# Self-attention of one decoder layer: both chunks of a query block handled together, products with the values and the query norms each in one run of column groups

## The chip, the cores and the metric

The kernel runs on one core of one Trainium2 chip. The metric is the device time of one execution in microseconds, from the runtime's own clock; the profile's span is the time from the first to the last instruction of the program within such an execution. PE is the matmul engine, PEld its weight load, DVE the vector engine, ACT the scalar engine, POOL the GpSimd engine, SP the engine that issues most DMAs.

## The reference

One inference step of one decoder layer for 256 prompt positions (two chunks of 128) and 8 sample requests of one position each, all in fp32. What is computed in sequence:

```
proj = rms_norm(x, g_mix) @ w_in                  # q | k | v | z | x,B,C | dt
q, k = rms_norm per head (16 and 4 heads of 64)
attn = sliding-window attention (window 128, a learned sink per head)
         prompt: each chunk sees itself and the chunk before, masked
         sample: one query per request against 128 cached rows and itself
ssd  = depthwise conv, SiLU, chunked state-space scan, gated norm
x = x + concat(attn, ssd) @ w_out
x = x + cross_attention(x, 256 memory tokens)     # 4 heads of 128
x = x + (silu(conv(gate)) * conv(value)) @ w_down # up-projection 2048 -> 2 x 5632
```

The prompt's attention, which the change concerns, is for each head `p = softmax(q k^T / 8 + mask, with the sink in the denominator)` and `o = p v`.

## The kernel before, in words

Positions lie along the free axis (256 prompt and 8 sample positions, 264 columns) and features along the partitions. All large products are done three times in a one-pass format: weights and inputs are split into a high and a low part, and `mm3` (L97 to L100) multiplies high by high, high by low and low by high into one accumulation. `weights` (L72) loads 128x1024 of a matrix, ACT casts the high part `whi` (L85), DVE subtracts it to get the remainder `wlo` (L86). `proj` (L102) does pairs of 128 output rows: 96 such products ("projection products" in what follows) for a pair of blocks with 2048 inputs.

The input projection comes in 26 pairs (`in_pair`, L350): keys, values, four pairs of queries, then the convolution's blocks (B and C, then x), then z. A pair's accumulators are two PSUM banks of tag "mm" (three banks), and from the sixteenth pair on every other one takes two of tag "t" (two banks, L355). The other tags are "s", "x" and "y" with a bank each.

Small products that are not of this kind are in fp32: the profile shows two records for each such product, one for a transpose. They are written for a few heads at a time and a scheduler that runs when the program is built puts them between the projection products, on each engine in one fixed order. That order, and not the code's, is what the chip runs; an engine that comes to an instruction whose inputs are not there stands still.

The query norm (L561 to L564): for each of 8 query blocks `j` (two heads each) ACT squares the block, and a product with a 128x32 selection matrix `nw` sums the squares of the two heads. Block `j` writes 32 partitions of bank "s" (column group `j % 4`), blocks 0 to 3 and 4 to 7 adding into the same four groups. `qn`, two transposes, a square root and a reciprocal make the factors `rqs` of it (L577 to L586).

The prompt's attention `attn_prompt` (L510) is called for each of 8 query blocks and treats each chunk `c` by itself: scores of both heads against 128 or 256 keys (L516, bank "s"), mask added by DVE (L519), maximum (L522), three small steps with the norm's factors and the sink (L524 to L526), exponentials on ACT (L527, L529), denominator (L531, L532), scaling (L534), transposes on PE (L539, shown as L271) into a "t" bank, a copy by ACT (L541, tile `pt`), the products with the values (L545: head 0 writes partitions 0 to 63, head 1 64 to 127 of another "t" bank) and a copy into `attn` (L547). The scores' tile `pe` has three buffers, shared under the tag "h0" with the sample's attention and the old states `h0` of `ssd_sample`; `pt` has two.

After it `attn_sample` (L591) does the 8 sample requests: scores in one bank "s" (L611), softmax (L615 to L623), a transpose into a "t" bank (L625), DVE's copy of it (L626), products with the cached values (L633), a copy (L635), a transpose and a diagonal product into the other "t" bank (L637, L638), and DVE's sums (L641, L645). `ssd_prompt` (L717) is the scan of the prompt, `ssd_sample` (L786) that of the sample requests: for each of 32 tiles a load of an old state on POOL's queue (L793), a product (L794) and a sum (L795) on DVE.

Of the kernel before, what the change touches and what calls it, by code (L numbers as in the profile page):

```python
# [7 lines left out]
F32 = mybir.dt.float32  # L8
F32R = mybir.dt.float32r
AF = mybir.ActivationFunctionType  # L10
ALU = mybir.AluOpType
AX = mybir.AxisListType
# [4 lines left out]
TP, TS = 256, 8  # L17
# [30 lines left out]
def hybrid_decoder_step_kernel(ctx: ExitStack, tc: tile.TileContext, I, O):  # L48
    nc = tc.nc
    V, S, P, PE = nc.vector, nc.scalar, nc.gpsimd, nc.tensor  # L50
# [9 lines left out]
    def psum(tag):  # L60
        return ps.tile([128, 512], F32, tag=tag, name=tag, bufs=banks[tag])

    def T3(pool, n, dt=F32, tag=None, name=None, bufs=None):
        return pool.tile([128, n, T], dt, tag=tag, name=name or tag, bufs=bufs)
# [191 lines left out]
    def pc(name, i=0, n=1):  # L256
        o = _PC[name][0]
        return par[:, o + i:o + i + n]
# [6 lines left out]
    maskb = cst[:, C_MASK:C_MASK + 256]  # L265
# [3 lines left out]
    def tr(out, in_):  # L269
        k = in_.shape[0]  # L270
        return PE.transpose(out, in_, cst[0:k, C_ID:C_ID + k])  # L271
# [59 lines left out]
    mp = mix.enter_context(tc.tile_pool(name="mp", bufs=1))  # L331
# [9 lines left out]
    def t32(name):  # L341
        return t6[:, next(t6n), :]
# [74 lines left out]
    vn = mp.tile([128, 2, 2, 128], F32, name="vn")  # L417
    p = psum("y")
# [20 lines left out]
    q = t32("q")  # L439
# [16 lines left out]
    p = psum("x")  # L456
# [5 lines left out]
    p = psum("x")  # L462
# [44 lines left out]
    nsink = mp.tile([128, 16], F32, name="nsink")  # L507
    V.tensor_scalar(out=nsink, in0=pc("sink_p", 0, 16), scalar1=-1.0, scalar2=None, op0=ALU.mult)

    def attn_prompt(j, rq, nrq):  # L510
        pp = j // 4
        for c in range(2):
            nk = 128 * (c + 1)
            p = psum("s")
            s3 = p[:, 0:2 * nk].rearrange("p (h k) -> p h k", h=2)
            PE.matmul(s3, qT[:, j, c * 128:c * 128 + 128], kbd[:, pp, :, 0:nk], start=True, stop=True)  # L516
            e = mp.tile([128, 2, 256], F32, tag="h0", name="pe", bufs=3)
            ev = e[:, :, 0:nk]
            V.tensor_tensor(out=ev, in0=s3, in1=maskb[:, 256 - nk:256].unsqueeze(1).broadcast_to([128, 2, nk]), op=ALU.add)  # L519
            st = mp.tile([128, 8], F32, tag="st", name="st", bufs=4)  # L520
            mx, den, es = st[:, 0:2], st[:, 2:4], st[:, 4:6]
            V.tensor_reduce(out=mx, in_=ev, op=ALU.max, axis=AX.X)  # L522

            V.tensor_tensor(out=mx, in0=mx, in1=nrq[:, c, :], op=ALU.mult)  # L524
            V.tensor_tensor(out=mx, in0=mx, in1=nsink[:, 2 * j:2 * j + 2], op=ALU.min)
            V.tensor_tensor(out=es, in0=mx, in1=pc("sink_p", 2 * j, 2), op=ALU.add)  # L526
            S.activation(out=es, in_=es, func=AF.Exp)  # L527
            for h in range(2):
                S.activation(out=e[:, h, 0:nk], in_=e[:, h, 0:nk], func=AF.Exp, scale=rq[:, c, h:h + 1], bias=mx[:, h:h + 1],  # L529
                             accum_out=den[:, h:h + 1])  # L530
            V.tensor_tensor(out=den, in0=den, in1=es, op=ALU.add)  # L531
            V.reciprocal(out=den, in_=den)  # L532
            for h in range(2):
                V.tensor_scalar(out=e[:, h, 0:nk], in0=e[:, h, 0:nk], scalar1=den[:, h:h + 1], scalar2=None, op0=ALU.mult)  # L534
            p = psum("t")
            nb = c + 1
            for h in range(2):
                for kb in range(nb):
                    tr(p[:, (h * nb + kb) * 128:(h * nb + kb) * 128 + 128], e[:, h, kb * 128:kb * 128 + 128])  # L539
            pt = mp.tile([128, 4, 128], F32, tag="bc", name="pt", bufs=2)  # L540
            S.copy(out=pt[:, 0:2 * nb, :], in_=p[:, 0:2 * nk].rearrange("p (a q) -> p a q", q=128))  # L541
            o = psum("t")
            for h in range(2):
                for kb in range(nb):
                    PE.matmul(o[64 * h:64 * h + 64, 0:128], vn[:, kb, pp, 64 * h:64 * h + 64], pt[:, h * nb + kb, :],  # L545
                              start=kb == 0, stop=kb == nb - 1)
            marks["attn"] = S.copy(out=attn[:, j, c * 128:c * 128 + 128], in_=o[:, 0:128])  # L547

    marks = {}

    qsq = [T3(apool, 4, tag="R", name=f"qsq{i}", bufs=4) for i in range(2)]
    nw = zz[:, :, 512:544]
# [6 lines left out]

            S.activation(out=qsq[j // 4][:, j % 4, :TP], in_=qT[:, j, :TP], func=AF.Square)  # L560
    pq = psum("s")  # L561
    for d in range(2):
        for j in range(4):
            PE.matmul(pq[32 * j:32 * j + 32, 0:TP], nw[:, d, :], qsq[d][:, j, :TP], start=d == 0, stop=d == 1)  # L564
    cpc = mp.tile([128, 24, 8], F32, name="cpc")
    ctmp = mp.tile([128, 2, TP], F32, tag="c", name="ctmp", bufs=2).rearrange("p a b -> p (a b)")[:, :192].rearrange("p (a b) -> p a b", b=8)

# [10 lines left out]
    pq = psum("x")  # L578
# [8 lines left out]
    for j in range(8):  # L587
        d = 2 * (j // 4)
        attn_prompt(j, rqs[:, :, j % 4, d:d + 2], nrqs[:, :, j % 4, d:d + 2])
# [109 lines left out]
    for c in range(2):  # L699
        p = psum("x")  # L700
# [4 lines left out]
    for w, XT in enumerate((BT, CT)):  # L705
        p = psum("x")
# [71 lines left out]
    p = psum("x")  # L778
# [196 lines left out]
    pts = [t.rearrange("p (m a q) -> p m a q", m=2, a=2) for t in (vp[:, 1024:2048], pp1[:, 0:1024])]  # L975
# [164 lines left out]
    p = psum("y")  # L1140
# [43 lines left out]
    for pi, (wh, wl) in enumerate(weights(I["w_co"][0])):  # L1184
        wh, wl = (w.rearrange("p (k c) -> p k c", c=512) for w in (wh, wl))
        for k in range(2):
            h = 2 * pi + k
# [7 lines left out]
    for u in range(1, 4):  # L1195
        proj([I["w_co"][u]], [(OH, OL)], lambda m, pm, u=u: x2_ev(4 * u + m, pm), nb=4,
             tag=[cyc[(4 * (u - 1) + m) % 5] for m in range(4)])
# [255 lines left out]
def build(shapes):  # L1453

    import concourse.bacc as bacc

    nc = bacc.Bacc("TRN2", target_bir_lowering=False, num_devices=1)
    ins = {n: nc.dram_tensor(f"in_{n}_dram", s, dt, kind="ExternalInput").ap() for n, (s, dt) in shapes.items()}
    outs = {n: nc.dram_tensor(f"out_{n}_dram", s, F32, kind="ExternalOutput").ap() for n, s in _OUTS}
    with tile.TileContext(nc, schedule_with_timeline_sim=True) as tc:  # L1460
        hybrid_decoder_step_kernel(tc, ins, outs)
    return nc
# [10 lines left out]
```

## Time and profile before

| what | value |
|---|---|
| device time, three runs | 1409.09, 1410.20, 1411.24 us (median 1410.2) |
| device time of the profiled execution | 1409.84 us |
| its span | 1407.8 us |
| L545, products with the values | 96 records, 8.8 us of busy time |
| L564, query norm | 16 records, 2.3 us of busy time |
| granted TensorE clock | 1.00 |

A line of the timeline gives the start, the duration, the engine, the line, what is written and read, the size and the number of records merged; a bracket at its end tells how long the engine had been idle and what ended that. A record of a matmul is longer than what it costs, since matmuls are pipelined and their records overlap: what one costs is read from the start of one to the start of the next.

### The profile page before, as it was taken

How to read it: one execution, taken by the hardware profiler on the slowest of the kernel's cores; microseconds unless marked ns; L12 is line 12 of the kernel's file. 1: busy time of each engine (PE TensorE's matmuls, PEld its weight loads, DVE VectorE, ACT ScalarE, POOL GpSimd, SP SyncE). 2: the span in 40 equal slices, each digit the busy share in tenths (PEclk: the TensorE clock that was granted, in tenths of full speed). 3: DMA queues.
4: the chain of work that ended last, by engine and by line, in shares of the span. 5: the costliest groups of instructions: out<-in, count | busy, mean ns of one | idle time of the engine just before them, and what ended most of it. 6: DMA issues, size and time to landing. Idle time of an engine off the chain costs nothing.

```text
span 1407.8 us, 29049 instructions
## 1 busy us (share of the span) xinstructions
PE 1399.9 (99%) x11525; PEld 1367.7 (97%) x11525; DVE 1047.8 (74%) x1909; ACT 764.1 (54%) x1255; POOL 96.2 (7%) x282
## 2 busy tenths in 40 slices
PE   9999999999999999999999999999999999999999
PEld 8998899999999999899999999999999999999999
DVE  7869879999997784468777775777577757765664
ACT  7557765656545554566565553555355535543432
POOL 0000001221010000020010010001000100000000
PEclk9999999999999999999999999999999999999999
DMA  8864357777776667666576765676567656656554
GB/s 300 290 191 134 118 178 251 223 249 249 243 225 236 188 224 246 247 232 192 178 235 235 238 230 182 212 242 228 181 211 229 206 182 198 199 175 191 183 188 139
DMA packets 90775, 298.33 MB, mean 212 GB/s; under 512 B 12304, under 2 KB 17808, under 8 KB 90128
## 3 DMA queue, kind: packets, MB, share of 16 engines
q1 hardware_dynamic: 84704, 277.34, 60.2%
q0 software_dynamic: 5504, 18.88, 4.2%
q8 instruction: 90, 1.47, 0.4%
q14 instruction: 45, 0.37, 0.1%
q10 hardware_dynamic: 432, 0.27, 0.1%
HBM read 280.77 MB, written 16.23 MB: 211 GB/s over the span
## 4 chain that ended last, share of the span: by engine, by line
PE 97%; DMA 1%; DVE 1%; issue 0%; ACT 0%; ACTq 0%; SPq 0%; DVEq 0%
PE mm L99 21%; PE mm L98 21%; PE mm L100 21%; PE t L99 10%; PE t L98 10%; PE t L100 10%; PE s L516 1%; PE t L271 1%; PE y L750 1%; PE t L545 1%; DMA cpast<-in_cpast_dram 1%; PE y L766 0%; DMA xT<-in_xT_dram 0%; PE t L242 0%; PE x L271 0%; PE x L1045 0%
## 5 line engine op out<-in xcount | busy, mean ns | idle before, releaser
L85 ACT CAST whi<-wraw 128x1024 fp32r<-128x1024 f32 x442 | 462.5, 1048 | 526.1 <-PE mm L99 271.2
L86 DVE TENSOR_TENSOR wlo<-wraw,whi 128x1024 fp32r<-128x1024 f32 x442 | 542.1, 1227 | 232.1 <-ACT whi L85 229.7
L98 PE MATMUL mm<-x2h,whi 128*128 128x264 f32 x704 | 199.8, 284 | 0.0
L98 PE MATMUL t<-x2h,whi 128*128 128x264 f32 x704 | 199.7, 284 | 0.0
L99 PE MATMUL t<-x2l,whi 128*128 128x264 f32 x704 | 199.7, 284 | 0.0
L99 PE MATMUL mm<-x2l,whi 128*128 128x264 f32 x704 | 199.6, 284 | 0.0
L100 PE MATMUL t<-x2h,wlo 128*128 128x264 f32 x704 | 199.5, 283 | 0.0
L100 PE MATMUL mm<-x2h,wlo 128*128 128x264 f32 x704 | 199.3, 283 | 0.0
L99 PE MATMUL mm<-hl,whi 128*128 128x264 f32 x704 | 198.7, 283 | 0.0
L100 PE MATMUL mm<-hh,wlo 128*128 128x264 f32 x704 | 198.2, 283 | 0.0
L98 PE MATMUL mm<-hh,whi 128*128 128x264 f32 x704 | 197.2, 284 | 0.0
L98 PE MATMUL mm<-xh,whi 128*128 128x264 f32 x608 | 176.3, 292 | 0.0
L99 PE MATMUL mm<-xl,whi 128*128 128x264 f32 x608 | 173.8, 287 | 0.0
L100 PE MATMUL mm<-xh,wlo 128*128 128x264 f32 x608 | 172.0, 288 | 0.4 <-DVE wlo L86 0.4
L99 PEld LDWEIGHTS t<-x2l,whi 128*128 128x128 f32 x704 | 132.5, 188 | 0.0
L99 PEld LDWEIGHTS mm<-x2l,whi 128*128 128x128 f32 x704 | 132.5, 188 | 0.0
L99 PEld LDWEIGHTS mm<-hl,whi 128*128 128x128 f32 x704 | 132.5, 188 | 0.0
L98 PEld LDWEIGHTS t<-x2h,whi 128*128 128x128 f32 x704 | 132.5, 188 | 0.0
L98 PEld LDWEIGHTS mm<-x2h,whi 128*128 128x128 f32 x704 | 132.4, 188 | 0.0
L100 PEld LDWEIGHTS t<-x2h,wlo 128*128 128x128 f32 x704 | 132.2, 188 | 0.0
L100 PEld LDWEIGHTS mm<-x2h,wlo 128*128 128x128 f32 x704 | 132.1, 188 | 0.0
L100 PEld LDWEIGHTS mm<-hh,wlo 128*128 128x128 f32 x704 | 131.9, 188 | 0.0
(461 smaller groups left out, 2917.9 us busy)
## 6 DMA issues: line engine op xcount, KB each, us to landing
wraw<-in_w_up_dram SPq DMA_DIRECT2D x176, 512.0 KB, 4.2
wraw<-in_w_in_dram SPq DMA_DIRECT2D x102, 512.0 KB, 4.8
wraw<-in_w_dn_dram SPq DMA_DIRECT2D x88, 512.0 KB, 4.2
wraw<-in_w_out_dram SPq DMA_DIRECT2D x48, 512.0 KB, 4.5
h<-in_h_dram POOLq DMA_DIRECT2D x32, 256.0 KB, 4.6
hn<-in_h_dram SPq DMA_DIRECT2D x16, 512.0 KB, 4.8
out_state_s_dram<-hn POOLq DMA_DIRECT2D x16, 512.0 KB, 3.9
e<-dram_la SPq DMA_DIRECT2D x16, 256.0 KB, 4.6
```

The costliest lines, as they stand in the source:

```text
L85: S.copy(out=hi, in_=x)
L86: V.tensor_tensor(out=lo, in0=x, in1=hi.bitcast(F32), op=ALU.subtract)
L98: PE.matmul(out, wh, xh, start=start, stop=False)
L99: PE.matmul(out, wh, xl, start=False, stop=False)
L100: PE.matmul(out, wl, xh, start=False, stop=stop)
L271: return PE.transpose(out, in_, cst[0:k, C_ID:C_ID + k])
L516: PE.matmul(s3, qT[:, j, c * 128:c * 128 + 128], kbd[:, pp, :, 0:nk], start=True, stop=True)
L545: PE.matmul(o[64 * h:64 * h + 64, 0:128], vn[:, kb, pp, 64 * h:64 * h + 64], pt[:, h * nb + kb, :], start=kb == 0, stop=kb == nb - 1)
L750: PE.matmul(y[o:o + 64, (h // 2) * 128:(h // 2) * 128 + 128], xdt[:, h, :], es[h // 4][:, h % 4, :], start=True, stop=True)
```

## The change

The change touches `attn_prompt` and the query norm. Both chunks of a query block go through together: the two score products write different banks ("s" for the first chunk, "y" for the second by the text `"ys"[c]`: "y" for c = 0, "s" for c = 1), the small steps on maximum, sink and denominator are done once for both chunks (four columns instead of two), the transposed probabilities of both chunks are held in the two `pt` buffers, and the products of both chunks with the values write one "t" bank and are issued in one run, six products without another one between. ACT copies the result once. The query norm's eight products are issued in one run as well, blocks 4 to 7 first. In the changed kernel the lines behind L510 move: scores L520, products with the values L556, query norm L578, and everything from `attn_sample` on by 21 (L615 becomes L636, L794 becomes L815).

```diff
     def attn_prompt(j, rq, nrq):
         pp = j // 4
+        st = mp.tile([128, 3, 2, 2], F32, tag="st", name="st", bufs=4)
+        mx, den, es = st[:, 0], st[:, 1], st[:, 2]
+        ev = []
         for c in range(2):
             nk = 128 * (c + 1)
-            p = psum("s")
+            p = psum("ys"[c])
...
-            V.tensor_tensor(out=mx, in0=mx, in1=nrq[:, c, :], op=ALU.mult)
-            V.tensor_tensor(out=mx, in0=mx, in1=nsink[:, 2 * j:2 * j + 2], op=ALU.min)
-            V.tensor_tensor(out=es, in0=mx, in1=pc("sink_p", 2 * j, 2), op=ALU.add)
-            S.activation(out=es, in_=es, func=AF.Exp)
+            V.tensor_reduce(out=mx[:, c, :], in_=e, op=ALU.max, axis=AX.X)
+            ev.append(e)
...
+        V.tensor_tensor(out=mx, in0=mx, in1=nrq, op=ALU.mult)
+        V.tensor_tensor(out=mx, in0=mx, in1=sink(nsink), op=ALU.min)
+        V.tensor_tensor(out=es, in0=mx, in1=sink(pc("sink_p", 0, 16)), op=ALU.add)
+        S.activation(out=es, in_=es, func=AF.Exp)
...
-            o = psum("t")
-            for h in range(2):
-                for kb in range(nb):
-                    PE.matmul(o[64 * h:64 * h + 64, 0:128], vn[:, kb, pp, 64 * h:64 * h + 64], pt[:, h * nb + kb, :],
-                              start=kb == 0, stop=kb == nb - 1)
-            marks["attn"] = S.copy(out=attn[:, j, c * 128:c * 128 + 128], in_=o[:, 0:128])
+            pts.append(pt)
+        o = psum("t")
+
+        def pv(c):
+            nb = c + 1
+            return [PE.matmul(o[64 * h:64 * h + 64, c * 128:c * 128 + 128], vn[:, kb, pp, 64 * h:64 * h + 64], pts[c][:, h * nb + kb, :],
+                              start=kb == 0, stop=kb == nb - 1) for h in range(2) for kb in range(nb)]
+
+        with tc.issue_after(pv(1)[0].ins):
+            pv(0)
+        marks["attn"] = S.copy(out=attn[:, j, 0:TP], in_=o[:, 0:TP])
...
-    for d in range(2):
+    def norm(d, j):
+        return PE.matmul(pq[32 * j:32 * j + 32, 0:TP], nw[:, d, :], qsq[d][:, j, :TP], start=d == 1, stop=d == 0)
+
+    with tc.issue_after(norm(1, 3).ins):
+        for j in range(3):
+            norm(1, j)
         for j in range(4):
-            PE.matmul(pq[32 * j:32 * j + 32, 0:TP], nw[:, d, :], qsq[d][:, j, :TP], start=d == 0, stop=d == 1)
+            norm(0, j)
```

The built program's order shows it. First PE's order at the products with the values of one query block; `pt` are the transposed probabilities, `vn` the values, numbers tell tiles apart. Before:

```order
L545 MATMUL t_1175<-pt_1173,vn_488 64x128 x2
L271 MATMUL t_1195<-cst_72,pe_1181 128x128 x4
L516 MATMUL s_1262<-kv_339,attn_347 128x256
L100 MATMUL mm_1889<-xh0_78,wlo_1893 128x264
...
L100 MATMUL mm_1889<-xh0_78,wlo_1899 128x264
L545 MATMUL t_1202<-pt_1200,vn_488 64x128 x4
L271 MATMUL t_1224<-cst_72,pe_1210 128x128 x2
L516 MATMUL s_1287<-kv_339,attn_347 128x512
```

Now:

```order
L100 MATMUL mm_1817<-xh0_78,wlo_1827 128x264
L556 MATMUL t_1182<-pt_1180,vn_488 64x128 x4
L556 MATMUL t_1182<-pt_1171,vn_488 64x128 x2
L520 MATMUL s_1241<-kv_339,attn_347 128x512
L520 MATMUL y_1281<-kv_339,attn_347 128x256
L98 MATMUL mm_1817<-xh0_78,whi_1826 128x264
```

The two runs, 25 projection products apart, are one, into one bank. Eight such runs stand in the changed program, the last after projection product 1287 (counting L98 to L100 from the start), where the last of before stood after 1026; the norm's eight products stand in one run too, where before six stood together and two alone.

Second, PE's order at the second half of the sample requests' attention; `es_e` are their probabilities, `vc` the cached values, `oss` the result before its transpose, `dgs` a diagonal. Before, at projection products 1149 to 1194:

```order
L271 MATMUL t_1570<-cst_72,es_e_1565 128x128
L98 MATMUL mm_2494<-xh1_80,whi_2563 128x264
...
L633 MATMUL s_1575<-vc_343,zz_345 32x128 x16
L100 MATMUL mm_2631<-xh0_78,wlo_2635 128x264
...
L271 MATMUL t_1594<-cst_72,oss_1592 128x128
L638 MATMUL t_1594<-dgs_1573,cst_72 128x128
L98 MATMUL mm_2631<-xh0_78,whi_2640 128x264
```

Now, at 1333 to 1344; `s_1471` are the scores:

```order
L632 MATMUL s_1471<-kcT_341,zz_345 32x129 x16
L99 MATMUL mm_2806<-xl1_81,whi_2875 128x264
...
L100 MATMUL mm_2806<-xh1_80,wlo_2876 128x264
L271 MATMUL t_1498<-cst_72,es_e_1493 128x128
L654 MATMUL s_1503<-vc_343,zz_345 32x128 x16
L271 MATMUL t_1522<-cst_72,oss_1520 128x128
L659 MATMUL t_1522<-dgs_1501,cst_72 128x128
L744 MATMUL s_2704<-CT_1535,BT_1534 128x128
L98 MATMUL t_2942<-xh0_78,whi_2946 128x264
```

The four steps of the sample, spread over 120 projection products from its scores on, now stand within 11, and the projection products behind them write the other bank of the same tag "t". 24 products on, PE transposes `xs0` into the bank that `x_2723` held (row `L271 MATMUL x_2767`).

Third, DVE's order behind DVE's copy of that transpose; `h0` are old states, `x_2723` the bank that PE wants next. Before:

```order
L626 COPY zz_345<-t_1570 128x4x4x8
...
L794 TENSOR_TENSOR h0_3165<-h0_3165,cb_3159 128x512
L670 SCALAR_TENSOR_TENSOR c_2617<-u2_545,par_71,c_2617 128x256
L795 TENSOR_REDUCE ych_2205<-h0_3165 128x4
L670 SCALAR_TENSOR_TENSOR c_2617<-u3_547,par_71,c_2617 128x256
L86 TENSOR_TENSOR wlo_2882<-wraw_2879,whi_2881 128x1024
L641 TENSOR_TENSOR tso_1597<-t_1594,kv_339 128x64 x2
```

Now:

```order
L647 COPY zz_345<-t_1498 128x4x4x8
L691 SCALAR_TENSOR_TENSOR c_2929<-u3_547,par_71,c_2929 128x256
L693 SCALAR_TENSOR_TENSOR xs2_2125<-xs2_2125,c_2929 128x2x256
L815 TENSOR_TENSOR h0_3089<-h0_3089,cb_3087 128x512
L815 TENSOR_TENSOR h0_3093<-h0_3093,cb_3087 128x512
L816 TENSOR_REDUCE ych_2133<-h0_3089 128x4
L816 TENSOR_REDUCE ych_2133<-h0_3093 128x4
L662 TENSOR_TENSOR tso_1525<-t_1522,kv_339 128x64 x2
L766 TENSOR_TENSOR xw_2730<-x_2723,de_535 128x512
L746 TENSOR_TENSOR s_2704<-s_2704,cst_72 128x128
L666 TENSOR_TENSOR tso_1525<-tso_1525,t_1522 128x128
```

The first steps of the scan (L766, L746) stand directly behind the sample's sums and the old states' first products, and the load of `h0_3093` waits for PE's transpose of the sample's probabilities (`t_1498`), whose buffer it takes over.

More of the change, by code (lines that the diff above doesn't have):

```diff
@@ L511, in attn_prompt @@
         pp = j // 4
+        st = mp.tile([128, 3, 2, 2], F32, tag="st", name="st", bufs=4)
+        mx, den, es = st[:, 0], st[:, 1], st[:, 2]
+        ev = []
         for c in range(2):
             nk = 128 * (c + 1)
-            p = psum("s")
+            p = psum("ys"[c])
             s3 = p[:, 0:2 * nk].rearrange("p (h k) -> p h k", h=2)
             PE.matmul(s3, qT[:, j, c * 128:c * 128 + 128], kbd[:, pp, :, 0:nk], start=True, stop=True)
-            e = mp.tile([128, 2, 256], F32, tag="h0", name="pe", bufs=3)
@@ L518, in attn_prompt @@
[L518 to L522, printed above, removed]
-            V.tensor_tensor(out=mx, in0=mx, in1=nrq[:, c, :], op=ALU.mult)
-            V.tensor_tensor(out=mx, in0=mx, in1=nsink[:, 2 * j:2 * j + 2], op=ALU.min)
@@ L526, in attn_prompt @@
-            V.tensor_tensor(out=es, in0=mx, in1=pc("sink_p", 2 * j, 2), op=ALU.add)
-            S.activation(out=es, in_=es, func=AF.Exp)
-            for h in range(2):
[L529 to L532, printed above, removed]
-            for h in range(2):
-                V.tensor_scalar(out=e[:, h, 0:nk], in0=e[:, h, 0:nk], scalar1=den[:, h:h + 1], scalar2=None, op0=ALU.mult)
@@ L535, in attn_prompt, with sink @@
-            p = psum("t")
+            e = mp.tile([128, 2, 256], F32, tag="h0", name="pe", bufs=3)[:, :, 0:nk]
+            V.tensor_tensor(out=e, in0=s3, in1=maskb[:, 256 - nk:256].unsqueeze(1).broadcast_to([128, 2, nk]), op=ALU.add)
+            V.tensor_reduce(out=mx[:, c, :], in_=e, op=ALU.max, axis=AX.X)
+            ev.append(e)
+        def sink(x):
+            return x[:, 2 * j:2 * j + 2].unsqueeze(1).broadcast_to([128, 2, 2])
+        V.tensor_tensor(out=mx, in0=mx, in1=nrq, op=ALU.mult)
@@ new lines, in attn_prompt @@
+        V.tensor_tensor(out=mx, in0=mx, in1=sink(nsink), op=ALU.min)
+        V.tensor_tensor(out=es, in0=mx, in1=sink(pc("sink_p", 0, 16)), op=ALU.add)
+        S.activation(out=es, in_=es, func=AF.Exp)
+        for c in range(2):
+            for h in range(2):
+                S.activation(out=ev[c][:, h, :], in_=ev[c][:, h, :], func=AF.Exp, scale=rq[:, c, h:h + 1], bias=mx[:, c, h:h + 1],
+                             accum_out=den[:, c, h:h + 1])
+        V.tensor_tensor(out=den, in0=den, in1=es, op=ALU.add)
@@ L536, in attn_prompt @@
+        V.reciprocal(out=den, in_=den)
+        pts = []
+        for c in range(2):
             nb = c + 1
             for h in range(2):
-                for kb in range(nb):
-                    tr(p[:, (h * nb + kb) * 128:(h * nb + kb) * 128 + 128], e[:, h, kb * 128:kb * 128 + 128])
-            pt = mp.tile([128, 4, 128], F32, tag="bc", name="pt", bufs=2)
-            S.copy(out=pt[:, 0:2 * nb, :], in_=p[:, 0:2 * nk].rearrange("p (a q) -> p a q", q=128))
-            o = psum("t")
+                V.tensor_scalar(out=ev[c][:, h, :], in0=ev[c][:, h, :], scalar1=den[:, c, h:h + 1], scalar2=None, op0=ALU.mult)
+            p = psum("t")
@@ L543, in attn_prompt @@
             for h in range(2):
                 for kb in range(nb):
-                    PE.matmul(o[64 * h:64 * h + 64, 0:128], vn[:, kb, pp, 64 * h:64 * h + 64], pt[:, h * nb + kb, :],
-                              start=kb == 0, stop=kb == nb - 1)
-            marks["attn"] = S.copy(out=attn[:, j, c * 128:c * 128 + 128], in_=o[:, 0:128])
+                    tr(p[:, (h * nb + kb) * 128:(h * nb + kb) * 128 + 128], ev[c][:, h, kb * 128:kb * 128 + 128])
+            pt = mp.tile([128, 4, 128], F32, tag="bc", name="pt", bufs=2)
@@ new lines, in attn_prompt @@
+            S.copy(out=pt[:, 0:2 * nb, :], in_=p[:, 0:256 * nb].rearrange("p (a q) -> p a q", q=128))
+            pts.append(pt)
[6 more added lines that the diff above has]
+            pv(0)
```

## The prediction

> **What bounds the kernel now.** I read the page first, then the waits of PE, then a table of two stretches, then the timeline of PE and DVE around the lines that the diff names.
>
> ```profile
> span 1407.8 us, 29049 instructions
> PE 1399.9 (99%) x11525; PEld 1367.7 (97%) x11525; DVE 1047.8 (74%) x1909; ACT 764.1 (54%) x1255; POOL 96.2 (7%) x282
> ```
> ```profile
> PE mm L99 <- DVE ohl L1132: 1.0, 1, 1.0
> ```
> ```profile
> 85.00:212.00 127.00, 127.00 (x1050) 114.98 (x1050) 104.65 (x299) 87.07 (x198) 3.40 (x6) 1.00 0.47 149
> 212.00:400.00 188.00, 188.00 (x1569) 181.83 (x1568) 185.62 (x356) 106.71 (x187) 34.62 (x42) 1.00 0.76 244
> ```
> PE idles 7.9 of 1407.8 us. Past the start its longest wait is the 1.0 us of L1132. Each microsecond that PE saves or newly waits therefore moves the end by one. The table (span, then busy time of PE, PEld, DVE, ACT, POOL) says where that could fail: from 85 to 212 us, where the self-attention lies, DVE has 22 us to spare, from 212 to 400 us only 2.4. Busy time of PE does not price a matmul, since records overlap. I price by start to start: what a run of other products adds between two products of the projection that would follow each other.
>
> ```profile
> 108.31 0.29 PE L98 MATMUL mm<-xh,whi 128*128 128x264 f32 x1
> 108.53 0.44 PE L545 MATMUL t<-pt,vn 128*64 128x128 f32 x4
> 108.90 0.39 PE L99 MATMUL mm<-xl,whi 128*128 128x264 f32 x1
> 109.12 0.28 PE L100 MATMUL mm<-xh,wlo 128*128 128x264 f32 x1
> ...
> 114.88 0.28 PE L98 MATMUL mm<-xh,whi 128*128 128x264 f32 x1
> 115.09 0.67 PE L545 MATMUL t<-pt,vn 128*64 128x128 f32 x8
> 115.69 0.39 PE L99 MATMUL mm<-xl,whi 128*128 128x264 f32 x1
> 115.91 1.02 PE L516 MATMUL s<-kv,attn 128*128 128x512 f32 x2
> ```
> ```profile
> 85.42 0.28 PE L100 MATMUL mm<-xh,wlo 128*128 128x264 f32 x1
> 85.63 1.06 PE L564 MATMUL s<-qsq,zz 128*32 128x256 f32 x12
> 86.62 0.39 PE L98 MATMUL mm<-xh,whi 128*128 128x264 f32 x1
> 86.84 0.28 PE L99 MATMUL mm<-xl,whi 128*128 128x264 f32 x1
> 86.96 0.28 PE L100 MATMUL mm<-xh,wlo 128*128 128x264 f32 x1
> ```
> ```profile
> 89.25 0.28 PE L98 MATMUL mm<-xh,whi 128*128 128x264 f32 x1
> 89.47 0.62 PE L564 MATMUL s<-qsq,zz 128*32 128x256 f32 x2
> 90.02 0.39 PE L99 MATMUL mm<-xl,whi 128*128 128x264 f32 x1
> 90.24 0.28 PE L100 MATMUL mm<-xh,wlo 128*128 128x264 f32 x1
> ```
> Two projection products follow each other at 0.12 us (86.84, 86.96). A product in fp32 leaves two records, so x4 is two products.
>
> **The change part by part. Runs of column groups.** A run's price is the time from the projection product before it to the second one behind it, less two steps of 0.12. The two products of a first chunk: 109.12 - 108.31 - 0.24 = 0.57 us. The four of a second chunk: 115.91 - 114.88 - 0.24 = 0.79. Two more products cost 0.22, so a run has a fixed 0.35, and two 64-column products share a round of 0.22. One run of six is then 0.79 + 0.22 = 1.01 instead of 0.57 + 0.79 = 1.36. Part of the fixed price is the longer step behind the run (0.22 between 108.90 and 109.12, not 0.12). Most first-chunk runs lead into transposes, where that 0.10 is paid once for the whole group; the pair then costs 1.26. So a head pair saves 0.25 to 0.35, eight save 2.0 to 2.8; I take 2.3, as most are of the cheaper sort.
>
> The query norm: six products in a run cost 86.84 - 85.42 - 0.24 = 1.18 (two rounds, the second half full), and each of the two lone ones 90.24 - 89.25 - 0.24 = 0.75. In one run, the eight fill the same two rounds: 1.18 instead of 2.68, saving 1.5. Together PE has **3.8 us less** (3.5 to 4.3) to do. The 48 transposes and the 16 products of L516 stay. DVE loses 40 small instructions, ACT 16; PE waited for none of them, so I cost them at nothing.
>
> **What the order makes of it.** A head pair now holds two of the three score buffers and both transposed ones, so fewer are under way at once, and the last run of products with the values stands after product 1287 of the projections instead of 1026. The sample queries' attention behind it moves from where pairs of "mm" banks alternate to the end of the fourteenth pair (product 1344). The next pair writes banks of tag "t", of which there are two, and the sample's transposes want the same two. So on PE the transpose of the sample's probabilities, its products with the cached values, the transpose of their result and the diagonal product now follow each other with nothing between. Before, 75 projection products stood ahead of the first of them and 20 or more between the next ones. Now 11 do: each step is a wait.
>
> ```profile
> 191.80 0.29 DVE L615 TENSOR_REDUCE sts<-s 128x1 f32<-128x129 f32 x1
> ...
> 192.47 1.22 DVE L86 TENSOR_TENSOR wlo<-wraw,whi 128x1024 fp32r<-128x1024 f32 x1
> 193.60 0.15 DVE L617 TENSOR_SCALAR sts<-sts 128x1 f32<-128x1 f32 x1
> 193.66 0.48 DVE L670 SCALAR_TENSOR_TENSOR c<-u,par,c 128x256 f32<-128x256 f32 x1
> 194.06 0.18 DVE L681 SCALAR_TENSOR_TENSOR ysam<-tsm,csm 128x32 f32<-128x32 f32 x1
> ...
> 197.58 0.28 DVE L623 TENSOR_SCALAR es_e<-es_e,sts 128x129 f32<-128x129 f32 x1
> ```
> ```profile
> 199.71 0.42 DVE L659 TENSOR_TENSOR u<-mm,r 128x264 f32<-128x264 f32 x1
> 200.06 0.28 DVE L626 COPY zz<-t 128x128 f32<-128x128 f32 x1
> ```
> *First wait.* From the sample's maximum to its normalised probabilities, DVE took 197.86 - 191.80 = 6.06 us, with three weight remainders (L86, 1.13 start to start), four steps of the convolution (L670, 0.40) and three small steps of about 0.11 between. In the new order two remainders, three convolution steps, an eviction (0.35, 199.71 to 200.06) and a copy of about 0.1 stand there: 6.06 - 1.13 - 0.40 - 0.33 + 0.45 = 4.65, and up to 0.3 for three small steps that now follow each other: 4.9. The maximum starts late too: ahead of it in DVE's order an eviction (0.35), a remainder (1.13) and a copy (0.1) begin when the score products do, so 1.65 us after their start.
>
> ```profile
> 201.43 1.08 PE L633 MATMUL s<-vc,zz 128*32 128x128 f32 x32
> 202.44 0.39 PE L100 MATMUL mm<-xh,wlo 128*128 128x264 f32 x1
> ```
> ```profile
> 202.58 0.27 ACT L635 COPY oss<-s 128x128 f32<-128x128 f32 x1 [0.36 <-PE s L633]
> ```
> ```profile
> 205.22 0.27 PE L271 MATMUL t<-cst,oss 128*128 128x128 f32 x1
> 205.34 0.39 PE L638 MATMUL t<-dgs,cst 128*128 128x128 f32 x2
> ```
> PE is through sixteen such products in 1.0 (L633 stands for the scores, of the same size), and with 11 projection products in 1.0 + 0.1 + 11 x 0.12 = 2.45. It waits until 1.65 + 4.9 = 6.55: **4.1 us**. Bounds: 3.5, were the remainder ahead done sooner; 5.3 with 6.06 for the chain.
>
> *Second.* The transpose (0.12), then DVE's copy of it, behind two convolution steps and the diagonal (0.4 + 0.2 + 0.4, then 0.28): PE waits **1.1** (0.5 to 1.4). *Third.* ACT's copy ended 202.85 - 201.43 = 1.42 after L633 began, PE was free after 1.0: **0.4**.
>
> ```profile
> 198.38 0.28 DVE L628 TENSOR_SCALAR dgs<-cst,es_e 128x128 f32<-128x128 f32 x1
> ```
> ```profile
> 199.22 0.54 POOL L793 DMA_DIRECT2D h<-in_h_dram  x1 [20.11 <-PE mm L100]
> ```
> ```profile
> 204.93 0.69 DVE L794 TENSOR_TENSOR h<-h,cb 128x512 f32<-128x512 f32 x1
> ```
> ```profile
> h<-in_h_dram POOLq DMA_DIRECT2D x32, 256.0 KB, 4.6
> L793 POOL DMA_DIRECT2D h<-in_h_dram x32: 538/538/585, 178.6 to 388.4; - x32
> ```
> *Fourth.* 24 products on, PE transposes a second block of the scan's inputs, whose bank DVE frees with L766. DVE has L766 behind two products with an old state (L815), two sums, and L662. The second state goes to the buffer that the sample's probabilities leave, so its load is issued only after the transpose and the diagonal. Before, the diagonal ended at 198.66 and the product stood at 204.93: 6.3 us; by the median landing it is 0.5 + 4.6 = 5.1. Then come that product and two sums of as many elements (0.69, or 0.6 start to start), two small ones of L662 (0.2 each) and L766, again 0.69: 3.0 in all (2.9 to 3.1). So L766 ends 8.1 to 9.3 after the diagonal, which itself ends 0.6 after the probabilities. PE by then has 0.1 + 1.1 + 1.0 + 0.4 + 0.6 + 24 x 0.12 = 6.1 from the probabilities: it waits 2.6 to 3.8. I take **2.9**, nearer to the median landing. *Fifth.* L744's mask, L666 and two L757 follow L766 on DVE; the scan's next products want the last: **0.5** (0 to 1).
>
> L793's issue took 538 to 585 ns in all 32 cases, though DVE was busy 185.6 of 188 us. The Trainium skill, page "SBUF — State Buffer" (section A bandwidth-pool intuition that's wrong), says that a DMA issued by GpSimd cannot get its descriptors written while DVE holds the shared port, 620 ns becoming 3100: by that page the fourth wait would be an estimated 2.5 us longer. The rows don't show it, and the sum leaves it out.
>
> Waits: 4.1 + 1.1 + 0.4 + 2.9 + 0.5 = 9.0 us. None has cover. Sum: 9.0 - 3.8 = +5.2. The profiled execution took 1409.84 us (2.0 around its span), 0.4 under the median of 1410.2. **Forecast: 1409.8 + 5.2 = 1415.0 us.** What this measurement can tell from no change is 0.2%, 2.8 us.
>
> **The rivals.** *Only the runs count (faster).* If the readiness of the sample's chain is better than its order says, the waits shrink; faster by over 0.2% needs them under 1.0 us in sum. At none it is 1406.0. Against it: the 11 products cover 1.3 us of a DVE chain with two remainders of 1.13 alone.
>
> *The loads come in time (the same).* The fourth and fifth waits go if L815 finds its state landed; the first three stay at 5.6: 1411.6. For it: in the whole trace DVE waited 0.4 us for these loads. Against it: their release now hangs on PE's transpose, and DVE has little else ahead.
>
> *A backlog on DVE (slower still).* The last head pair and the sample's chain now fall into the stretch in which DVE has 2.4 us to spare. A pair's mask, maximum and scaling are three passes over 768 columns (1.0 each by the 0.69 of 512), the chain 4.9: 7.9 - 2.4 = 5.5 us of late evictions if the waits don't let DVE catch up: 1420.5. For it: 185.62 of 188. Against it: while PE stands still in the first wait, DVE works, and the 40 small instructions saved were 0.15 each (193.60).
>
> *A slower clock after the wait.* The granted clock is 1.00 in both stretches of the table, but past the start no wait was over 1.0 us. Were it halved for as long as the first wait lasts, 4.1 us of work would take 2.0 more: 1417. The Trainium skill, page "TensorE: Matmul & The Clock Gate" (Part 1), says that an idle window of about 3.4 us halves the clock; no run here shows it.
>
> *The runs are not formed.* The order excludes it: six products stand in a row eight times, eight once.
>
> **How the numbers follow.** Forecast 0.52; loads in time 0.17; backlog 0.15; clock 0.08; only the runs 0.08. The low end, 1410.0, takes in most of the same case, the high end, 1420.5, the backlog and the long ends of the waits; what is left out is the faster case and the tails. Faster 0.08, same 0.17, slower 0.75; slower alone has 1413.1 to 1420.5.
>
> **What would show it.** PE idle of some 17 us instead of 7.9, the new part in five gaps within 20 us of each other at the end of the sample's attention, ended by DVE's probabilities, DVE's copy, ACT's copy and L766; runs of 12 records of L556 followed 1.0 us later; 16 records of L578 in one run. It is wrong if PE's idle time stays under 10 us, or if the gaps lie elsewhere, at the transposes of a head pair or, long after, at evictions.

## The result, and the profile after

The changed kernel took 1418.63 us (median of 4 runs, 1416.76 to 1419.08), the kernel before 1409.78 us (median of 4) beside it: 1.006 times as long, 95% interval 1.0048 to 1.0071. It is slower by 8.9 us, where 5.2 were forecast. The page of the changed kernel:

```profile
span 1417.3 us, 28981 instructions
PE 1400.7 (99%) x11525; PEld 1370.8 (97%) x11525; DVE 1045.5 (74%) x1869; ACT 762.6 (54%) x1239; POOL 94.9 (7%) x282
```

PE idles 16.6 us, 8.7 more than before, though its busy time rose by only 0.8. Its waits say where:

```profile
PE t L271 <- DVE es_e L644: 6.5, 1, 6.5
PE mm L99 <- DVE ohl L1153: 1.7, 1, 1.7
...
PE s L744 <- DVE e L757: 0.9, 1, 0.9
PE s L654 <- DVE zz L647: 0.7, 1, 0.7
...
PE y L771 <- DVE e L757: 0.5, 1, 0.5
...
PE t L271 <- ACT oss L656: 0.4, 1, 0.4
```

Three of the five forecast waits are here under their own names: the sample's probabilities (6.5), DVE's copy (0.7), ACT's copy (0.4), all between 218 and 229 us. The fourth, on L766, is missing, and at the place of the fifth, the scan's first products, PE does not wait either. The two waits on L757 (0.5 and 0.9) end at 248.8 and 262.4 us, at later steps of the scan, which the forecast had not priced. The five add up to 9.0 us, as the forecast ones did, but by other shares. The table of stretches (span, then busy time of PE, PEld, DVE, ACT, POOL, then the granted clock) shows what else was paid:

```profile
210.00:218.50 8.50, 8.50 (x91) 7.95 (x91) 3.17 (x12) 8.44 (x20) 0.00 (x0) 1.00 0.24 86
218.50:225.03 6.53, 0.05 (x2) 0.07 (x1) 6.36 (x17) 4.99 (x11) 0.00 (x0) 0.78 0.46 146
225.03:232.30 7.27, 6.20 (x51) 5.49 (x52) 4.09 (x10) 0.90 (x2) 1.08 (x2) 0.50 0.51 160
232.30:262.00 29.70, 28.68 (x238) 26.72 (x237) 27.33 (x56) 16.01 (x32) 6.54 (x11) 1.00 0.65 204
```

From within the long wait (mean 0.78) to 232.3 us the granted clock is 0.50. The 6.2 us that PE worked there would have taken 3.1: the clock cost 3.1 us, as the rival of the slower clock had it, which had a chance of 8% and a price of 2.0.

What PE saved can be read too. One of the new runs by itself, and the norm:

```profile
195.59 0.28 PE L98 MATMUL mm<-xh,whi 128*128 128x264 f32 x1
195.80 0.88 PE L556 MATMUL t<-pt,vn 128*64 128x128 f32 x12
196.61 0.39 PE L99 MATMUL mm<-xl,whi 128*128 128x264 f32 x1
196.84 0.28 PE L100 MATMUL mm<-xh,wlo 128*128 128x264 f32 x1
```
```profile
89.33 0.29 PE L99 MATMUL mm<-xl,whi 128*128 128x264 f32 x1
89.55 1.07 PE L578 MATMUL s<-qsq,zz 128*32 128x256 f32 x16
90.55 0.51 PE L100 MATMUL mm<-xh,wlo 128*128 128x264 f32 x2
90.90 0.30 PE L98 MATMUL mm<-xh,whi 128*128 128x264 f32 x1
```

The run of six: 196.84 - 195.59 - 0.24 = 1.01 us, as forecast. The norm: 90.90 - 89.33 = 1.57, less three steps of 0.12 (the x2 are two products): 1.21, where 1.18 were forecast. Priced in the same way and summed over all runs from 80 to 440 us, what PE does between projection products took 59.7 us before. In the changed kernel it took 67.6; without the five waits (9.0) and the 1.9 us that half the clock added to the sample's five steps (3.8 us, 1.9 before), 56.7 are left, 3.0 less than before where 3.8 were forecast. The rest went to lone transposes: a head pair's now often stand by themselves between projection products (30 such runs instead of 9, 5.4 us instead of 2.3), and each pays the lead again.

The account closes, in the profiled executions (1419.08 and 1409.84 us), over the stretch in which both kernels differ, from the 300th to the 3200th projection product (starts of the records of L98 to L100): 413.3 us before, 422.4 after, 9.1 more = 9.0 of waits + 3.1 of slow clock - 3.0 saved.

### The profile page after: what moved, and what is told of

Same layout as the page of the kernel before. It is cut to its first block, busy times and chain, and to the rows that moved or that the text cites. A ratio compares the mean times of both kernels' runs of the same rounds, so it can differ in the third digit from the quotient of the medians.

```text
span 1417.3 us, 28981 instructions
## 1 busy us (share of the span) xinstructions
PE 1400.7 (99%) x11525; PEld 1370.8 (97%) x11525; DVE 1045.5 (74%) x1869; ACT 762.6 (54%) x1239; POOL 94.9 (7%) x282
## 4 chain that ended last, share of the span: by engine, by line
PE 93%; DMA 2%; DVE 2%; issue 1%; ACT 1%; POOL 0%; ACTq 0%; SPq 0%; POOLq 0%; DVEq 0%
PE mm L99 20%; PE mm L98 20%; PE mm L100 20%; PE t L98 9%; PE t L99 9%; PE t L100 9%; PE s L520 1%; DVE wlo L86 1%; PE t L271 1%; DMA cpast<-in_cpast_dram 0%; PE t L556 0%; PE y L771 0%; DMA cb<-dram_bc 0%; PE y L787 0%; DMA xT<-in_xT_dram 0%
## 5 line engine op out<-in xcount | busy, mean ns | idle before, releaser
L98 PE MATMUL t<-x2h,whi 128*128 128x264 f32 x704 | 199.8, 284 | 0.0
L98 PE MATMUL mm<-x2h,whi 128*128 128x264 f32 x704 | 199.8, 284 | 0.0
L100 PE MATMUL t<-x2h,wlo 128*128 128x264 f32 x704 | 199.5, 283 | 0.0
L100 PE MATMUL mm<-x2h,wlo 128*128 128x264 f32 x704 | 199.4, 283 | 0.0
L100 PE MATMUL mm<-hh,wlo 128*128 128x264 f32 x704 | 198.2, 283 | 0.0
L98 PE MATMUL mm<-hh,whi 128*128 128x264 f32 x704 | 197.2, 284 | 0.0
L98 PE MATMUL mm<-xh,whi 128*128 128x264 f32 x608 | 175.7, 291 | 0.0
L100 PE MATMUL mm<-xh,wlo 128*128 128x264 f32 x608 | 173.2, 289 | 0.1
L98 PEld LDWEIGHTS t<-x2h,whi 128*128 128x128 f32 x704 | 132.5, 188 | 0.0
L98 PEld LDWEIGHTS mm<-x2h,whi 128*128 128x128 f32 x704 | 132.4, 188 | 0.0
L100 PEld LDWEIGHTS t<-x2h,wlo 128*128 128x128 f32 x704 | 132.2, 188 | 0.0
L100 PEld LDWEIGHTS mm<-x2h,wlo 128*128 128x128 f32 x704 | 132.1, 188 | 0.0
L100 PEld LDWEIGHTS mm<-hh,wlo 128*128 128x128 f32 x704 | 132.0, 188 | 0.0
```

The source lines that it names most:

```text
L98: PE.matmul(out, wh, xh, start=start, stop=False)
L100: PE.matmul(out, wl, xh, start=False, stop=stop)
```

## The experiments

Theory A: the loss is the waits at the sample's steps and the slow clock behind them. Its rivals: a backlog that the longer attention leaves on DVE (B), and, formed later, the small steps done for both chunks at once (C) and a next place where DVE and not PE sets the time (D). All medians have 5 to 11 runs where nothing else is said, and the ratio is to the kernel before on the same chip.

**e1: the next pair writes "mm" banks.**

```diff
-proj(..., tag="t" if i > 13 and i % 2 else "mm")
+proj(..., tag="t" if i > 15 and i % 2 else "mm")
```

> The changed kernel, but the first pair of projection blocks that writes the two banks of tag "t" is the eighteenth, no longer the sixteenth; the sixteenth takes "mm" banks. PE's order up to the sample's scores stays, and then some 100 projection products stand between the scores and the sample's second products instead of 11. Theory A (the loss is PE's waits where the sample's four steps hold the banks that the next pair wants, and the slow clock behind them): the waits of 6.5, 0.7 and 0.4 us, about 3 us of half-speed work behind them and the 1.4 us at the scan go, so 1418.6 - 12 = about 1407, under the kernel before by 2 to 4 us. Theory B (attention in whole pairs loads DVE with a backlog): the evictions come late all the same, 1414 or more.

It took 1416.65 us (1.0045, 1.0032 to 1.0057), 2.0 less than the changed kernel, not 12. PE's waits:

```profile
PE x L271 <- DVE xw L766: 3.1, 1, 3.1
PE mm L98 <- ACT whi L85: 1.9, 1, 1.9
...
PE y L771 <- DVE hp L793: 0.8, 1, 0.8
```

The waits at the sample's steps are gone, all of them: the shared banks were their cause. But 3.1, 0.8 and 1.9 us of new ones stand at 375 to 386 us, at the end of the scan, and half clock from 375 to 382:

```profile
375.07:381.80 6.73, 5.85 (x33) 5.12 (x34) 6.73 (x16) 1.12 (x3) 1.63 (x3) 0.50 0.79 208
```

Theory A had the place and the mechanism right, and was wrong that nothing would follow. Between 85 and 240 us DVE was busy for 124.5 us in e1 and for 132.6 in the kernel before, while PE had come further (1503 projection products by 240 us, 1439 before), and over the whole run DVE has only 1.0 us less to do (1046.8, 1047.8). So DVE enters the scan with some 7 us of work still to be done, an estimate from these numbers. That it made this up in the changed kernel while PE stood still at 220 us fits, but is argued and not shown.

**e2: PE kept busy in the long wait.**

```diff
...
+        with tc.issue_after(last.ins):
+            for k in range(warm):
+                PE.matmul(outs[0][:, 264:512], A[0][0][:, k % 8, 0:128], A[0][0][:, 0, 0:248], start=True, stop=True)
...
```

`warm` is 40 for the fifteenth pair and 0 for all others. The lines behind the edit move by three (L644 becomes L647).

> The changed kernel with 40 further products of 248 columns, whose results nothing reads, put where PE waits for the sample's probabilities. They write free columns of a bank that is already evicted, so they run inside the 6.5 us wait and leave about 1.5 us of it. Theory A1 (the long wait itself halves the granted clock behind it): the clock stays at 1.00, the work from the probabilities on goes at full speed, 3 us less: about 1415.5, if no other wait shows up behind. Rival A2 (the clock falls for another reason, or the half-speed work lies beside other waits): 1418 to 1419, the wait only moves to the scan's transposes.

It took 1422.52 us (1.0082, 1.0070 to 1.0095).

```profile
PE y L291 <- DVE accy L867: 2.4, 1, 2.4
...
PE t L274 <- DVE es_e L647: 1.4, 1, 1.4
```
```profile
218.00:227.70 9.70, 7.62 (x89) 6.88 (x81) 8.20 (x21) 7.22 (x15) 0.00 (x0) 1.00 0.40 126
227.70:231.10 3.40, 3.04 (x39) 2.58 (x31) 2.41 (x7) 0.90 (x2) 0.84 (x2) 0.50 0.57 184
```

The wait was cut to 1.4 us and the clock stayed at 1.00 through it, so it is the idle time that lowers the clock; it fell only for the 3.4 us behind, after 1.4 + 0.4 us of idle close together. From the 300th to the 1400th product this gained 1.8 us on the changed kernel. All of it and more went again later: 2.4 us at the sum of the gate's squares (435.7 us), with half clock behind, and 1.6 in two others. Rival A2 came nearer, though not at the place that it named.

**e3: the sample's attention at high priority.**

```diff
-    attn_sample()
+    with tc.high_priority():
+        attn_sample()
```

> The changed kernel with the sample's attention at high priority in the order: its scores come 10 projection products earlier, and on DVE the maximum stands directly behind the convolution's last product instead of behind an eviction and a weight remainder too. Theory A (the first wait is the length of DVE's queue from the scores to the probabilities): 1.2 us by the ten products and about 1.6 by the eviction and the remainder, so the wait falls from 6.5 to 3.5 or 4 and the time to 1415 or 1416, and to 1413 if the clock then stays up. Rival (the chain waits for ACT and not for DVE's queue): the wait stays over 5.5 us and the time over 1417.5.

It took 1419.13 us (1.0063, 1.0050 to 1.0076).

```profile
PE t L271 <- DVE es_e L644: 5.1, 1, 5.1
PE x L271 <- DVE xw L767: 1.5, 1, 1.5
```

The wait fell by 1.4 us, about the ten products' worth (1.2), not by 2.8: the maximum still stood behind the convolution's last product, which waited for ACT. The total did not fall. The second row is the fourth wait of the prediction, on the step that is L766 in the changed kernel: here the clock was back at 1.00 by 227.6 us, so PE came early enough to meet it.

**e4 and e11: only the norm in one run** (the kernel before with the diff's last part; e11 is the same kernel once more, and its gate is not moved, whatever its label says).

> The kernel before with only the query norm in one run. By the price of the runs PE saves 1.5 us: 1408.3. Rival: the norm's one run starts only when all eight squares are there, the attention behind it moves back by some 80 projection products, and a new wait eats the gain: 1409.8 or more.

> A second look at the kernel of e4 (the kernel before with only the norm in one run), for the place of its wait: theory D has it again at the sum of the gate's squares, 4.0 us, with half clock behind it.

e4 took 1414.11 us (1.0028, 1.0017 to 1.0039), e11 1416.09 (one run). The run itself costs 1.21 us there as well, so 1.5 are saved, and yet e4 is 4.1 us slower than the kernel before beside it. PE's longest wait, in e4's profiled execution (1416.87 us, the longest of its seven):

```profile
PE y L288 <- DVE accy L850: 4.0, 1, 4.0
```

It lies at 424 to 428 us, 330 us behind the edit, at the sum of the gate's squares; in e11 it is 4.8. The order of everything behind the norm had been made anew, and the last products with the values stand at projection product 1111 instead of 1026.

**e5: small steps for each chunk again.** The products with the values stay in one run of six, the norm in one run.

```diff
-        V.tensor_tensor(out=mx, in0=mx, in1=nrq, op=ALU.mult)
...
-        V.tensor_tensor(out=den, in0=den, in1=es, op=ALU.add)
-        V.reciprocal(out=den, in_=den)
+            V.tensor_tensor(out=mx, in0=mx, in1=nrq[:, c, :], op=ALU.mult)
...
+            V.tensor_tensor(out=den, in0=den, in1=es, op=ALU.add)
+            V.reciprocal(out=den, in_=den)
```

> The changed kernel with one part undone: the small steps on maximum, sink and denominator are done for each chunk by itself again, so a chunk's exponentials, scaling and transposes need not wait for the other chunk; both chunks' products with the values are still in one run into one bank, and the norm in one run. In the order the last run with the values then stands at projection product 1031 (1287 in the changed kernel, 1026 before) and the sample's steps at 1082 to 1199, as before. Theory C (the loss comes from the steps done for both chunks at once: a pair holds its two scores' buffers longer, fewer chunks are on their way, DVE stands idle 7 us more during the attention, and behind the sample, where it has 2.3 us of idle time in 170 to 190, it can't make that up, so PE waits somewhere): the waits go and the saving of 3.8 us stays, 1406. Rival (the one run of six, with both transposed buffers held, is what holds the chunks up): 1411 or more.

It took 1409.81 us (1.0002, 0.9993 to 1.0011): 8.8 less than the changed kernel, as fast as before, but not 1406. The attention is back in its place, with the last run at product 1031. What the shared steps did is seen on DVE, in the stretch from 85 us to the last products with the values (span, then busy time of PE, PEld, DVE). First of the kernel before, then of the changed one, then of e5:

```profile
85.00:182.00 97.00, 97.00 (x759) 85.66 (x758) 80.11 (x240) 65.77 (x159) 1.26 (x2) 1.00 0.44 141
```
```profile
85.00:210.00 125.00, 125.00 (x1021) 117.21 (x1021) 100.96 (x250) 79.23 (x163) 1.26 (x2) 1.00 0.48 153
```
```profile
85.00:178.00 93.00, 93.00 (x759) 85.38 (x758) 78.79 (x238) 65.01 (x152) 1.25 (x2) 1.00 0.48 146
```

DVE stood idle 16.9, 24.0 and 14.2 us in them. In the changed kernel 8.6 us of it are one step, the sum of the denominators, which waits for the exponentials of both chunks:

```profile
DVE st L538 <- ACT pe L536: 5.8, 5, 2.2
...
DVE st L538 <- ACT st L533: 2.8, 2, 1.7
```

Before, that step's waits were:

```profile
DVE st L531 <- ACT st L527: 0.4, 2, 0.2
```

So a head pair takes some 94 projection products instead of 52 (629 to 1287 for seven of them, 664 to 1026 before), the attention ends 28 us later, and the sample's steps move to where the next pair wants their banks. Theory C holds for the attention: with the small steps apart, it is back in its place, though the run of six is kept. So its rival, that the run of six holds the chunks up, falls. Where the 3.8 us went that e5 should have kept, two waits at 421 to 424 us show, with half clock from inside the second of them to some 430 us:

```profile
PE mm L99 <- DVE yl L93: 1.9, 1, 1.9
...
PE mm L98 <- ACT yh L93: 0.5, 1, 0.5
```
```profile
423.30:429.50 6.20, 5.45 (x25) 5.46 (x26) 3.45 (x8) 0.43 (x2) 0.00 (x0) 0.50 0.67 215
```

This profiled execution took 1412.06 us, 2.3 more than e5's median. Four of the eleven show a mean clock of 1.000 and took 1407.6 to 1409.3 us, so what is lost here differs from one execution to the next.

**e6 to e8: less work on DVE.** In e1's kernel, the changed kernel and the kernel before:

```diff
-                V.tensor_tensor(out=h0, in0=h0, in1=cb, op=ALU.mult)
+                if i < 2:
+                    V.tensor_tensor(out=h0, in0=h0, in1=cb, op=ALU.mult)
```

> The kernel of e1 (sixteenth pair in "mm" banks), with the product of the old state left out for half of the 32 tiles of the sample requests' scan, so part of that result is not computed: DVE has 16 times 0.6 = 9.6 us less to do, nearly all of it behind the sample's attention. Theory C (DVE's sum of work from the attention to the scan's end is what PE waits for): the waits of 3.1, 0.8 and 1.9 us at the scan's end and the 6.7 us of half clock behind them (3.4 us) go: 1416.7 - 9.2 = 1407.5. Rival (those waits are local, a step of the scan behind its own releaser): 1414 or more.

> The changed kernel with the same half of the products with the old states left out, so part of that result is not computed. The first wait lies ahead of nearly all of that work: by theory C and theory A alike it stays at about 6.5 us with its half clock, and only the 1 to 2 us of waits at the scan can go: 1416.5 to 1418.5. Rival (the long wait is only DVE's backlog showing): it shrinks, 1412 or less.

> The kernel before with the same half of the products left out, so part of that result is not computed: the control. PE waits for DVE nowhere there, so 1409 to 1411, no change. If it gets faster by more than 1.5 us, DVE was already a bound before, and e6 tells less.

e6 took 1412.83 us (1.0023, 1.0014 to 1.0032), 3.1 above the kernel before beside it where e1 was 6.6 above; that is between theory C's 1407.5 and the rival's 1414. Its waits at the scan's end were 1.9, 0.9 and 0.7 instead of 3.1, 0.8 and 1.9. e7 took 1420.4 (1.0078, 1.0065 to 1.0091): the first wait stayed at 6.5, as the theories said, and others of 1.4 and 1.1 us came up. The control did not stay where it was expected: e8 took 1415.03 (1.0039, 1.0025 to 1.0052), slower by 5 us with less to do. Its longest wait is new, with half clock behind it:

```profile
PE t L98 <- DVE u L816: 3.6, 1, 3.6
```

Leaving work out makes a new order too, and here that cost 5 us. So the three don't tell how much of e1's waits is DVE's sum of work; e6 only fits it.

**e9 and e10: the gate's chain on POOL.** In e5 the two waits are for the split of the sample's gate, whose steps stand in DVE's order with weight remainders between them. Six of them go to POOL, in e5's kernel (e9) and in the kernel before (e10):

```diff
-        V.tensor_tensor(out=ych, in0=ych, in1=dsb[:, :, 8:16], op=ALU.mult)
-        V.tensor_tensor(out=ysam, in0=ysam, in1=ych, op=ALU.add)
+        P.tensor_tensor(out=ych, in0=ych, in1=dsb[:, :, 8:16], op=ALU.mult)
+        P.tensor_tensor(out=ysam, in0=ysam, in1=ych, op=ALU.add)
...
```

> The kernel of e5 with six of the products and sums of the sample requests' gate, between the scan's end and the output projection's second half, on POOL instead of DVE; all that is computed stays. In e5 PE is through with the first half earlier and waits 0.5 and 1.9 us there for the split of this gate's result, which ends at 424.0 us as before. Theory D (PE's saving of 3.8 us is real and was lost at the next place where a chain on DVE, and not PE, sets the time): without the six steps, and the weight remainders that stand between them in DVE's order, the split comes some 3 us sooner, the waits of 2.4 us and the half clock behind them go: 1406 to 1407, under the kernel before. Rival (another wait takes its place): 1409 or more.

> The control of e9: the kernel before with the same six steps on POOL. Before, PE waits for nothing there, so 1409 to 1411. If it is faster by over 1.5 us, the gain of e9 is not the runs'.

e9 took 1406.48 us, 0.9978 of the kernel before (0.9969 to 0.9986): faster than both kernels, as forecast. e10 took 1409.89 (1.0001, 0.9992 to 1.0010): no change. So moving these steps to POOL gains nothing by itself. The split L93 on DVE, first in e5, then in e9:

```profile
423.77 0.35 DVE L93 TENSOR_TENSOR yl<-ysam,yh 128x64 fp32r<-128x64 f32 x2
```
```profile
415.60 0.35 DVE L93 TENSOR_TENSOR yl<-ysam,yh 128x64 fp32r<-128x64 f32 x2
```

In e5 it ended at 424.1 us, with PE waiting; in e9 it is done at 415.95, and PE does not wait. From the 300th to the 3200th product e9 takes 409.8 us, 3.5 less than before, and in it PE's products between the projection's take 56.0 instead of 59.7. So of the 3.8 us that the prices of the runs gave, 3.7 are found again in PE's own work, 3.5 in this stretch, and 3.0 in the whole time (1409.52 before, beside it).

**e12: the norm alone, with the same steps on POOL.**

> The kernel of e4 (the kernel before with only the norm in one run) with the gate's six steps on POOL, as in e9. In e4 PE waits 4.0 us at the sum of this gate's squares and works at half clock behind it. Theory D: that wait goes, and the norm's saving of 1.5 us shows: 1408 to 1409. Rival (the norm's one run costs more than it saves, by its wait for all eight squares): 1411 or more.

It took 1408.47 us (0.9991, 0.9982 to 1.0000): 1.3 less than before (forecast 1.5), where the norm alone without it lost 4.1. The interval reaches 1.0000, so the gain itself is barely clear of no change; the loss is gone, and with it the wait at the gate's squares.

## Why the prediction was right, and where it was off

**Direction and range.** Slower, with a chance of 0.75; 1418.6 lies in 1410.0 to 1420.5. The likeliest, 1415.0, was 3.6 too low: the slow clock (3.1) had been left out of the sum, and 0.8 less was saved. That the waits came to 9.0 us as forecast is luck in part: the first was 2.4 us longer, the second 0.4 shorter, the fourth (2.9) and the fifth (0.5) did not come, and 1.4 us of waits at later steps of the scan had not been forecast. Of the sign that the prediction gave, five gaps within 20 us, three came, within 4 us of each other; the other two lie 20 and 34 us behind them.

**The price of the runs.** Right: 1.01 and 1.21 measured for 1.01 and 1.18. What the forecast left out is that the transposes would be scattered: 3.0 saved instead of 3.8. In e9, where they are not, it is 3.7 in PE's own work.

**First wait, 4.1 forecast, 6.5 measured.** This term was mis-sized by 2.4 us, and the fault is in the start of the chain. On DVE:

```profile
217.61 0.69 DVE L693 SCALAR_TENSOR_TENSOR xs<-xs,c 128x512 f32<-128x512 f32 x1 [1.34 <-ACT xs L692]
218.22 0.42 DVE L680 TENSOR_TENSOR u<-mm,r 128x264 f32<-128x264 f32 x1
218.56 1.21 DVE L86 TENSOR_TENSOR wlo<-wraw,whi 128x1024 fp32r<-128x1024 f32 x1
219.69 0.16 DVE L687 COPY cnew<-u 128x11 f32<-128x11 f32 x1
219.77 0.28 DVE L636 TENSOR_REDUCE sts<-s 128x1 f32<-128x129 f32 x1
...
224.56 0.28 DVE L644 TENSOR_SCALAR es_e<-es_e,sts 128x129 f32<-128x129 f32 x1
```
```profile
215.89 1.09 PE L632 MATMUL s<-kcT,zz 128*32 128x129 f32 x32
```

From the maximum to the probabilities it took 224.84 - 219.77 = 5.07 us (forecast 4.9). But the maximum started 3.9 us after the score products (215.89), not 1.65: DVE came to the eviction ahead of it late, since the convolution's last product, one place further ahead (L693), waited for ACT. I had counted what stands directly ahead of the chain and not what that waits for.

**Second and third, 1.1 and 0.4 forecast:** 0.7 and 0.4.

**Fourth, 2.9 forecast, none measured.** The mechanism was there, on DVE:

```profile
230.90 0.69 DVE L815 TENSOR_TENSOR h<-h,cb 128x512 f32<-128x512 f32 x1 [2.49 <-DMA h<-in_h_dram]
231.50 1.27 DVE L816 TENSOR_REDUCE ych<-h 128x4 f32<-128x512 f32 x2
232.69 0.35 DVE L662 TENSOR_TENSOR tso<-t,kv 128x64 f32<-128x64 f32 x2
232.96 0.68 DVE L766 TENSOR_TENSOR xw<-x,de 128x512 f32<-128x512 f32 x1
```

DVE waited 2.5 us for the old state, and L766 ended at 233.64, 8.8 us after the probabilities (8.7 to 9.9 forecast). PE was to be there after 6.1; at half clock it came after 8.9 (233.74), and found it just done. One cost covered the other. In e3 and e7, where the clock was back sooner (227.6 and 229.6 us instead of 232.3), the wait shows (1.5 and 1.4).

**Fifth, 0.5 forecast, none measured at its place.** At 234.7 us, the first L771 behind L766, PE does not wait. The 0.5 and 0.9 us on L757 belong to later L757 steps, at 248.0 and 261.1 us on DVE.

**The rivals.** The slower clock, at 8%, is what happened, together with the forecast and not in place of it. The Trainium skill, page "TensorE: Matmul & The Clock Gate" (Part 1), gave the halving after some 3.4 us of idle time. By it a first wait of 4.1 was already long enough. I gave it little weight because no wait of before was long enough to show it, which is no evidence against it. The backlog on DVE, at 15%, is not what made the long waits of the changed kernel, which lie at the sample's steps; with those waits gone (e1), 5.8 us of waits come at the scan's end instead, near to the 5.5 that the rival gave, and DVE then has some 7 us of work still to be done at 240 us; both speak for it. How much of these is DVE's sum of work and how much the new order stays open (e6 to e8).

**What I had not seen.** That the sample's attention comes late at all was read from the order and taken as given. Its cause is the small steps done for both chunks at once, as e5 shows. The prediction counted them as 40 small DVE instructions less and put their effect on the time at nothing. They make DVE wait 8.6 us for exponentials, where before it was 0.4, and push the attention's end back by 28 us.

## What to carry to other kernels

Where one engine is busy to 99% and the others follow it in fixed orders, a saving on that engine counts only up to the next place where a chain on another engine sets the time: price the saving, then look for that place, which in e4 lay some 330 us behind the edit. Joining steps of two independent pieces of work saves instructions and makes each piece wait for the slower one; on an engine that works in order, that wait stops everything queued behind it. And a wait on PE can cost more than itself, by the half clock behind it: here 3.1 us on top of 6.5.

## What the runs showed of the hardware that was not expected

In these traces the half clock comes in stretches of about 3.4 us or two or three times that. Two of them, in the changed kernel and in e4:

```profile
222.10:232.30 10.20, 6.25 (x51) 5.56 (x52) 7.02 (x18) 2.29 (x4) 1.08 (x2) 0.50 0.54 171
```
```profile
426.86:433.70 6.84, 5.66 (x23) 5.46 (x24) 4.36 (x12) 2.15 (x4) 0.00 (x0) 0.50 0.66 181
```

In all it was 10.2 us (222.1 to 232.3) in the changed kernel, 6.8 in e3 (220.7 to 227.6), 6.8 in e4 (426.9 to 433.7), 6.8 in e1 (375.1 to 381.9), 3.4 each time in e2. The length does not follow the wait: behind the same wait of 6.5 us it was 10.2 us in the changed kernel and 6.8 in e7 (222.7 to 229.6), and behind 4.8 us in e11 it was 3.4 (428.6 to 432.0). The start varies too: the clock fell 2.4 us after PE's wait began in e3 (218.3, 220.7) and 4.3 us after it in e11 (424.3, 428.6). It doesn't take a wait as long as such a stretch: 2.4 us were enough in e2 (435.7 us), and 1.4 + 0.4 close together; a wait of 1.9 us by itself (e1, 386 us) and one of 1.7 (L1153 in the changed kernel) left the clock at 1.00. The Trainium skill, page "TensorE: Matmul & The Clock Gate" (Part 1), states that the clock halves after an idle window of about 3.4 us. On the idle time that it takes the traces differ: 2.4 us of idle time were enough in e2 and in e3.
